# Hybrid decoder layer on one core: raw buffers of v by name and rising order, gate loads behind the first V products, two more U steps in the selection

## The chip, the cores and the metric

The kernel runs on one core of a Trainium2 chip. The metric is the device time of one execution in microseconds. The core has TensorE (PE, its weight loads as PEld), VectorE (DVE), ScalarE (ACT), GpSimd (POOL) and SyncE (SP), which here only issues DMAs. Each engine, and SyncE's DMA queue, works through its own instructions in order.

## The reference, cut to what matters

The layer first mixes tokens (two groups of mixers, of which nothing changes here) and then runs PEER: each of 512 tokens selects, for each of 8 heads, 16 of 16384 experts by product keys, and sums `gelu(x . u_i) * gate_i * v_i` over its 128 experts.

```python
s = jnp.einsum('thpd,hpkd->thpk', q, sub_keys).astype(f32)
top_s, top_i = lax.top_k(s, K)
cand_s = (top_s[:, :, 0, :, None] + top_s[:, :, 1, None, :]).reshape(T, H, K * K)
best_s, best_pos = lax.top_k(cand_s, K)
expert_idx = jnp.take_along_axis(cand_i, best_pos, axis=-1)
gate = jax.nn.softmax(best_s, axis=-1)
...
act = jnp.einsum('td,ted->te', x_blk, u[i_blk]).astype(f32)
hid = jax.nn.gelu(act, approximate=False) * g_blk
return jnp.einsum('te,ted->td', hid.astype(v.dtype), v[i_blk])
```

## The kernel before

Three of the four token tiles (384 tokens) are computed densely: for each of 128 blocks of 128 experts a U step makes all products of the block with the tokens, the gates (zero where an expert is not selected) multiply them, and a V step multiplies with v's block and adds up in PSUM. The fourth tile gathers its own rows of u and v with indirect DMAs (`gather`, on GpSimd's queue), and VectorE works them off (`use`).

Matrix products are made from a high and a low half of each operand, three matmuls for each product (`mm3`, lines 108 to 110). ScalarE makes the high half; the low half is a subtraction on VectorE, or on GpSimd where `split` is told so (line 104). A U step is `u_part` 0 to 7, three matmuls each. At part 0 and part 4 `rhs_part` asks for the load of the U block two steps on (`us.loads`, two raw buffers, tile ur) and splits half a block of the next one (tiles uh and ul). `keep` closes a step: gelu on ScalarE and, for tokens whose gates are there, a multiplication with the gate row in `ring`, on VectorE.

The order of the work is written out by hand, engine by engine. It has these stages here.

- The selection. VectorE finds the best keys and turns them to indices (`select`, one call for a tile of tokens, with a tree of additions over tile gat); `spread` transposes indices and gates on TensorE, `spread2` copies them out of PSUM. Between these calls stand U steps (`u_run`), and ScalarE writes broadcast copies (`ties`, `piece`). In this stage GpSimd makes the low halves of U.
- The gate stage, 48 units of 8 tokens (`gunit`). VectorE makes one-hot tiles A, eq and B (`gprep`), TensorE 16 matmuls of them (tile pg), which give the dense gates of 8 tokens for all 128 blocks. The gates of the first 59 blocks go to `ring` in SBUF, those of the other 69 to a stage buffer, which after every 8 units is written to DRAM (tile gd, a DMA of ScalarE's queue). Between the units stand U parts, spread evenly so that all but two of the steps up to block 58 are done at the end. In this stage VectorE makes the low halves of U.
- The turn. The pool with A, eq, B and the stage buffers is closed. A new one is opened over its memory (`vp`) for the halves of v, the halves of the gate rows (hh and hl) and four raw buffers of v (tile vr). Two U steps stand here (the two `u_run(1)`), the first loads and splits of v, and `hprep(0)`, which splits gate row 0.
- The loop over the blocks e = 0 to 127 of v. A step has six groups of V products (18 matmuls) and, as long as there are any, one U step, of block 59 + e (24 matmuls). `vs.loads(e + 4)` asks for the raw block four steps on, `gload` reads a gate row of a block from 59 on back from DRAM into the place in `ring` that is free. `vs.split`, `hprep` make the halves for the next step.

A raw buffer may be loaded again when both halves of the block in it have been made. A load into memory that another tile held before waits for the last user of that tile. All loads of u, v, gate rows and constants go through SyncE's queue, so each waits behind the ones issued before it.

Of the kernel before, what the change touches and what calls it, by code (L numbers as in the profile page):

```python
# [7 lines left out]
F32 = mybir.dt.float32  # L8
# [10 lines left out]
D = 1024  # L19
# [16 lines left out]
class Stream:  # L36
# [9 lines left out]

    def loads(s, upto):
        while s.nl <= min(upto, len(s.src) - 1):
            s.raw[s.nl] = s.c.tile([128, 1024], F32, name=s.nm + "r", bufs=s.nraw)
            s.y.load(s.raw[s.nl], s.src[s.nl])  # L50
            s.nl += 1

# [11 lines left out]
class Layer:  # L64
# [31 lines left out]
    def tt(self, out, x, y, op):  # L96
        return self.V.tensor_tensor(out, x, y, op=op)  # L97
# [758 lines left out]
    def experts(self):  # L856
# [4 lines left out]
        c = ctx.enter_context(tc.tile_pool(name="ex", bufs=1, reuse_waits="tile"))  # L861
        NE, RS = 128, RING
# [7 lines left out]
        us = self.us  # L870
# [99 lines left out]
        def piece():  # L970
            t, o, i = pieces.pop(0)
            act(o, i, AF.Copy)

        def select(t):

            while any(p[0] == t for p in pieces):
                piece()
            ii = kp.tile([128, 2, 8, 16], F32, name="ii", bufs=2)
            for e in range(2):
                oh = c.tile([128, 8, 16, 16], F16, name="gat", tag="gat", bufs=3)  # L980
                tt(oh, bc(CF[0][:, e, t], 2, 16), bc(itj if e else its, 1, 8), OP.is_equal if e else OP.is_ge)
                tt(oh, oh, TIE[t][:, e], OP.mult)
                for n in (8, 4, 2):
                    tt(oh[:, :, 0:n, :], oh[:, :, 0:n, :], oh[:, :, n:2 * n, :], OP.add)
                tt(ii[:, e], oh[:, :, 0, :], oh[:, :, 1, :], OP.add)
            IX[t] = ii
# [24 lines left out]
        def spread(t):  # L1011
            ii, g = IX.pop(t), bs[:, t]
            p = pt()
            T.transpose(p[:, 0:128], flat(ii[:, 0]), ident)
            T.transpose(p[:, 128:256], flat(ii[:, 1]), ident)
            T.transpose(p[:, 256:384], flat(g), ident)
            act(gs[:, 0, t * 128:(t + 1) * 128], p[:, 256:384], AF.Copy, scale=SC)
            SPR[t] = p
# [29 lines left out]
        def u_part(i, pool=False):  # L1048
            e = nu[0]
            if e >= NE:  # L1050
                return
            if i == 0:
                up[0] = pt()
            self.rhs_part(up[0][:, :TD], tsd, not hold[0] and nu[0] < RS - 4)
            if i in PP and pieces:
                piece()
            if i == 7:
                keep(e, up[0])
                nu[0] += 1

        def u_run(n):
            for _ in range(n):
                for i in range(8):
                    u_part(i)
# [27 lines left out]
        ties(2)  # L1092
        u_run(1)
        select(1)
        spread(0)
        u_run(1)
        ties(3)
        select(2)
        u_run(2)
# [4 lines left out]
        select(3)  # L1104
        u_run(2)
        spread(2)
        u_run(4)
        spread2(2)
        idx = c.tile([128, 128], I32, name="idx")
        gt0 = c.tile([128, 128], F32, name="gt0")  # L1110
# [118 lines left out]
        vp = ctx.enter_context(tc.tile_pool(name="vp", bufs=1, reuse_waits="tile"))  # L1229
        vs = Stream(self, vp, "v", [a["v"][e * 128:(e + 1) * 128, :] for e in range(NE)], 4)  # L1230
        HT[0] = htile()
        vs.loads(1)
        u_run(1)
        vs.split(1)
        hprep(0)
        u_run(1)
        vs.loads(3)

        g0 = ng[0]
        share = [0]  # L1240
# [6 lines left out]
        hs = {}  # L1247

        def gload(e):
            if e < NE:  # L1250
                load(ring[:, e % RS, :], gd3[:, e - RS, :])

        gload(RS)

        def final():

            nv = lambda: c.tile([128, 4], F32, name="rs3", bufs=4)
            hf = [slice(0, 512), slice(512, 1024)]
            junk = [c.tile([128, D], F32, name="gat", tag="gat", bufs=3), vp.tile([128, D], F32, name="vr", bufs=4)]
            v = [nv() for _ in range(4)]  # L1260

            def products(t):
                s = slice(t * 128, t * 128 + 128)
                for n in range(2):
                    for e in (NE - 2, NE - 1):
                        self.mm3(pv[t][n], HT[e][0][:, s], HT[e][1][:, s], *vs.parts[2 * e + n], False, e == NE - 1)

            def residual(t, n):
                h = hs[t][:, hf[n]]
                stt(h, pv[t][n], 1.0 / SC, h, OP.mult, OP.add)  # L1270
                square(t, n)

            def square(t, n):
                act(junk[t % 2][:, hf[n]], hs[t][:, hf[n]], AF.Square, accum_out=v[t][:, n:n + 1])

            def weight(t, n, eng):
                eng.tensor_tensor(hs[t][:, hf[n]], hs[t][:, hf[n]], wf[:, hf[n]], op=OP.mult)

            def mean(t):
                V.tensor_scalar(v[t][:, 2:3], v[t][:, 0:1], EPS * D, None, op0=OP.add)  # L1280
                V.tensor_scalar(v[t][:, 0:1], v[t][:, 1:2], v[t][:, 2:3], 1.0 / D, op0=OP.add, op1=OP.mult)

            def power(t):
                G.tensor_tensor(v[t][:, 3:4], v[t][:, 0:1], self.mhalf, op=OP.pow)

            def scale(t):
                stt(hs[t], hs[t], v[t][:, 3:4], wf, OP.mult, OP.mult)
                load(self.out[t], hs[t])

            square(3, 0)  # L1290
            square(3, 1)
            mean(3)
            power(3)
            for t in range(3):
                products(t)
            residual(0, 0)
            residual(0, 1)
            scale(3)
            mean(0)
            power(0)  # L1300
            residual(1, 0)
            weight(1, 0, G)
            residual(1, 1)
            weight(1, 1, G)
            scale(0)
            mean(1)
            power(1)
            residual(2, 0)
            weight(2, 0, G)
            residual(2, 1)  # L1310
            weight(2, 1, V)
            act(hs[1], hs[1], AF.Copy, scale=v[1][:, 3:4])
            load(self.out[1], hs[1])
            mean(2)
            power(2)
            act(hs[2][:, hf[0]], hs[2][:, hf[0]], AF.Copy, scale=v[2][:, 3:4])
            V.tensor_scalar(hs[2][:, hf[1]], hs[2][:, hf[1]], v[2][:, 3:4], None, op0=OP.mult)
            load(self.out[2], hs[2])

        for e in range(NE):  # L1320
            todo = [gather] * (plan[e + 1] - plan[e])
            pos = [(2 * i + 1) * 7 // max(1, 2 * len(todo)) for i in range(len(todo))]

            def fill(i, todo=todo, pos=pos):
                while pos and pos[0] <= i:
                    pos.pop(0)
                    todo.pop(0)()

            vs.loads(e + 4)
            if e == NE - 2:  # L1330

                hprep(e + 1)
                vs.split(2 * e + 2)
                vs.pair = us.pair
                vs.split(2 * e + 3)
                final()
                break
            hh, hl = HT.pop(e)

            def vgrp(n, t):  # L1340
                s = slice(t * 128, t * 128 + 128)
                vh, vl = vs.parts[2 * e + n]
                self.mm3(pv[t][n], hh[:, s], hl[:, s], vh, vl, e == 0, e == NE - 1)

            for i in range(3):
                vgrp(0, i)
                if i == 2:
                    vs.parts.pop(2 * e)
                    vs.split(2 * e + 2)
                    hprep(e + 1)  # L1350
                    gload(e + 1 + RS)
                u_part(i)
                fill(i)
            u_part(3)
            for i in range(3):
                vgrp(1, i)
                if i == 2:
                    vs.parts.pop(2 * e + 1)
                    vs.split(2 * e + 3)
                u_part(4 + i)  # L1360
                fill(3 + i)
            u_part(7)
            fill(6)
            if e == NE - 12:
                for t in (0, 1):
                    hs[t] = us.c.tile([128, D], F32, name="ur", bufs=2)
                    load(hs[t], self.hd[t])
            if e == NE - 4:
                while ng[0] < 256 or pend:
                    gather()  # L1370
                vs.loads(NE - 1)
                wf = c.tile([128, D], F32, name="gat", tag="gat", bufs=3)
                load(wf, a["w_norm_final"].to_broadcast([128, D]))
                hs[2] = c.tile([128, D], F32, name="gat", tag="gat", bufs=3)
                load(hs[2], self.hd[2])
                hs[3] = acc[0]
# [90 lines left out]
```

## Time and profile before

| | us |
|---|---|
| median of 3 runs | 1524.52 |
| lowest, highest | 1524.38, 1526.88 |
| profiled execution, its own time | 1525.01 |
| its span in the trace | 1523.2 |
| TensorE busy in the span | 1479.2 (97%) |
| VectorE busy | 1168.4 (77%) |
| ScalarE busy | 632.3 (42%) |
| GpSimd busy | 451.6 (30%) |

The profile comes from one execution. Its own time contains the span, from the first instruction to the last, and about 1.8 us around it. Matmuls are pipelined, so the busy time of TensorE says when it had work, not that it ran at its peak. Idle time in front of an instruction stands in square brackets with what ended it. A q behind an engine's name means its queue or sequencer.

### The profile page before, as it was taken

How to read it: one execution, taken by the hardware profiler on the slowest of the kernel's cores; microseconds unless marked ns; L12 is line 12 of the kernel's file. 1: busy time of each engine (PE TensorE's matmuls, PEld its weight loads, DVE VectorE, ACT ScalarE, POOL GpSimd, SP SyncE). 2: the span in 40 equal slices, each digit the busy share in tenths (PEclk: the TensorE clock that was granted, in tenths of full speed). 3: DMA queues.
4: the chain of work that ended last, by engine and by line, in shares of the span. 5: the costliest groups of instructions: out<-in, count | busy, mean ns of one | idle time of the engine just before them, and what ended most of it. 6: DMA issues, size and time to landing. Idle time of an engine off the chain costs nothing.

```text
span 1523.2 us, 22401 instructions
## 1 busy us (share of the span) xinstructions
PE 1479.2 (97%) x7904; PEld 1290.1 (85%) x7904; DVE 1168.4 (77%) x2473; ACT 632.3 (42%) x1201; POOL 451.6 (30%) x380
## 2 busy tenths in 40 slices
PE   7999999999988999989999999999999999999997
PEld 6777767888988999878999999999889998888886
DVE  6543654599999999977777777787788788888886
ACT  5335633433653544433333333333333333444444
POOL 1002403444564000002333333333243333334332
PEclk9999999999999999999999999999999999999999
DMA  5231213322334556658889888889889897888894
GB/s 186 83 125 56 70 53 131 108 84 90 105 110 140 157 150 169 180 180 301 317 304 322 317 307 303 318 309 316 297 317 316 314 322 257 293 301 301 298 327 178
DMA packets 148738, 335.56 MB, mean 220 GB/s; under 512 B 64640, under 2 KB 73872, under 8 KB 148496
## 3 DMA queue, kind: packets, MB, share of 16 engines
q1 hardware_dynamic: 58672, 186.32, 36.0%
q0 software_dynamic: 36864, 134.23, 24.6%
q10 hardware_dynamic: 53088, 13.57, 3.8%
q8 instruction: 62, 1.02, 0.3%
q14 instruction: 52, 0.43, 0.1%
HBM read 315.79 MB, written 18.28 MB: 219 GB/s over the span
## 4 chain that ended last, share of the span: by engine, by line
PE 53%; issue 20%; DVE 13%; POOL 9%; DMA 3%; ACT 2%; POOLq 0%; SPq 0%; DVEq 0%; ACTq 0%
PE pm L108 16%; PE pm L109 16%; PE pm L110 16%; POOL gat L1133 8%; DVE gat L97 4%; PE pg L1184 2%; DVE ul L104 1%; DVE B L97 1%; PE pm L902 1%; DMA gd<-stage 1%; DVE ring L97 1%; DVE eq L97 1%; DVE A L97 1%; ACT b L91 1%; DMA gat<-in_u,idx 1%
## 5 line engine op out<-in xcount | busy, mean ns | idle before, releaser
L108 PE MATMUL pm<-nT,uh 128*128 128x384 f32 (+1 forms) x1152 | 404.3, 351 | 8.6 <-ACT uh L91 8.1
L109 PE MATMUL pm<-nT,uh 128*128 128x384 f32 (+1 forms) x1152 | 399.1, 346 | 0.5 <-DVE nT L97 0.5
L110 PE MATMUL pm<-nT,ul 128*128 128x384 f32 (+1 forms) x1152 | 397.5, 345 | 1.1 <-POOL ul L104 0.9
L109 PE MATMUL pm<-vl,hh 128*128 128x512 f32 x765 | 301.5, 394 | 1.2 <-DVE vl L104 1.2
L110 PE MATMUL pm<-vh,hl 128*128 128x512 f32 x765 | 300.9, 393 | 0.0
L108 PE MATMUL pm<-vh,hh 128*128 128x512 f32 x765 | 300.6, 393 | 0.2 <-ACT vh L91 0.2
L1133 POOL DMA_INDIRECT gat<-in_u,idx x128 | 137.8, 1076 | 477.6 <-DVE gat L100 470.3
L91 ACT ACTIVATE uh<-ur 128x512 fp32r<-128x512 f32 x288 | 180.2, 629 | 219.3 <-PE pm L109 185.9
L108 PEld LDWEIGHTS pm<-nT,uh 128*128 128x128 f32 x1152 | 218.0, 189 | 34.3 <-ACT uh L91 8.6
L109 PEld LDWEIGHTS pm<-nT,uh 128*128 128x128 f32 x1152 | 217.7, 189 | 25.4 <-DVE nT L97 1.1
L110 PEld LDWEIGHTS pm<-nT,ul 128*128 128x128 f32 x1152 | 217.8, 189 | 8.7 <-POOL ul L104 2.6
L1133 POOL DMA_INDIRECT gat<-in_v,idx x128 | 148.4, 1159 | 256.1 <-DVE n2a L100 223.1
L91 ACT ACTIVATE vh<-vr 128x512 fp32r<-128x512 f32 x255 | 159.5, 626 | 136.9 <-PE pm L110 136.9
L104 DVE TENSOR_TENSOR vl<-vr,vh 128x512 fp32r<-128x512 f32 x255 | 175.2, 688 | 33.5 <-ACT vh L91 33.0
L104 DVE TENSOR_TENSOR ul<-ur,uh 128x512 fp32r<-128x512 f32 x206 | 140.7, 689 | 61.5 <-ACT uh L91 61.3
L100 DVE SCALAR_TENSOR_TENSOR n2a<-gat,dots,n2a 128x1024 f32<-128x1024 f32 x128 | 163.9, 1280 | 24.2 <-DMA gat<-in_v,idx 19.2
L110 PEld LDWEIGHTS pm<-vh,hl 128*128 128x128 f32 x765 | 143.5, 188 | 32.7 <-DVE hl L104 0.3
L100 DVE SCALAR_TENSOR_TENSOR gat<-gat,n2a 128x1024 f32<-128x1024 f32 x128 | 156.1, 1220 | 13.9 <-DMA gat<-in_u,idx 13.7
L109 PEld LDWEIGHTS pm<-vl,hh 128*128 128x128 f32 x765 | 143.9, 188 | 15.6 <-DVE vl L104 1.9
L108 PEld LDWEIGHTS pm<-vh,hh 128*128 128x128 f32 x765 | 144.0, 188 | 14.2 <-ACT vh L91 0.7
L104 POOL TENSOR_TENSOR ul<-ur,uh 128x512 fp32r<-128x512 f32 x82 | 116.5, 1427 | 101.3 <-ACT uh L91 101.2
L91 ACT ACTIVATE gl<-pm 128x384 f32<-128x384 f32 (+16 forms) x104 | 46.0, 442 | 223.8 <-PE pm L110 223.8
(254 smaller groups left out, 1709.2 us busy)
## 6 DMA issues: line engine op xcount, KB each, us to landing
ur<-in_uT SPq DMA_DIRECT2D x128, 512.0 KB, 5.9
vr<-in_v SPq DMA_DIRECT2D x128, 512.0 KB, 5.5
gd<-stage ACTq DMA_DIRECT2D x6, 2208.0 KB, 14.7
ring<-gd SPq DMA_DIRECT2D x69, 192.0 KB, 5.6
wraw<-in_w_in SPq DMA_DIRECT2D x23, 512.0 KB, 4.3
ur<-in_w_query SPq DMA_DIRECT2D x16, 512.0 KB, 3.6
b<-in_x SPq DMA_DIRECT2D x8, 512.0 KB, 3.7
wraw<-in_w_out SPq DMA_DIRECT2D x8, 512.0 KB, 3.9
```

Source lines behind the costliest of these rows:

```text
L91: return self.S.activation(out, in_, f, **k)
L97: return self.V.tensor_tensor(out, x, y, op=op)
L100: return self.V.scalar_tensor_tensor(out, x, s, y, op0=op0, op1=op1, **k)
L104: (self.G if pool else self.V).tensor_tensor(lo, src, hi.bitcast(F32), op=OP.subtract)
L108: T.matmul(out, lhi, rhi, start=start, stop=False)
L109: T.matmul(out, lhi, rlo, start=False, stop=False)
L110: T.matmul(out, llo, rhi, start=False, stop=stop)
L902: T.matmul(p[:, t * 128:(t + 1) * 128], q[:, t * 128:(t + 1) * 128], skT[:, b, :], start=True, stop=True)
L1133: G.indirect_dma_start(out=r, out_offset=None, in_=src, in_offset=bass.IndirectOffsetOnAxis(ap=idx[:, k:k + 1], axis=0))
L1184: T.matmul(o, A[:, t // 2, :, t % 2], B[:, i, t // 2, :, t % 2], start=i == 0, stop=i == 1)
```

## The change

The raw buffers of v and u get names of their own (vr0 to vr3, ur0 and ur1), each with one buffer, in place of one name with four or two buffers; two users at the end follow. Three blocks of v are asked for ahead of the two U steps of the turn, in place of two ahead and two behind; step 0 asks for none beyond them, and step 1 then asks for blocks 3 to 5. The gate rows 59 and 60 are read back near the end of step 0, in place of row 59 ahead of the loop and row 60 in the middle of step 0. In the selection, the U step behind `spread(0)` is put ahead of it and one more with it, and the last run has five steps for four; the gate stage, which does what is left up to block 56, then has two steps less.

```diff
     def loads(s, upto):
         while s.nl <= min(upto, len(s.src) - 1):
-            s.raw[s.nl] = s.c.tile([128, 1024], F32, name=s.nm + "r", bufs=s.nraw)
+            s.raw[s.nl] = s.c.tile([128, 1024], F32, name=f"{s.nm}r{s.nl % s.nraw}", bufs=1)
             s.y.load(s.raw[s.nl], s.src[s.nl])
...
         select(1)
+        u_run(2)
         spread(0)
-        u_run(1)
         ties(3)
...
         spread(2)
-        u_run(4)
+        u_run(5)
         spread2(2)
...
         HT[0] = htile()
-        vs.loads(1)
+        vs.loads(2)
         u_run(1)
         vs.split(1)
         hprep(0)
         u_run(1)
-        vs.loads(3)
...
-        gload(RS)
-
...
-            junk = [c.tile([128, D], F32, name="gat", tag="gat", bufs=3), vp.tile([128, D], F32, name="vr", bufs=4)]
+            junk = [c.tile([128, D], F32, name="gat", tag="gat", bufs=3), vp.tile([128, D], F32, name=f"vr{NE % 4}", bufs=1)]
...
-            vs.loads(e + 4)
+            vs.loads(e + 4 if e else 2)
...
-                    gload(e + 1 + RS)
+                    if e:
+                        gload(e + 1 + RS)
...
+            if e == 0:
+                gload(RS)
+                gload(RS + 1)
             u_part(7)
...
-                    hs[t] = us.c.tile([128, D], F32, name="ur", bufs=2)
+                    hs[t] = us.c.tile([128, D], F32, name=f"ur{t}", bufs=1)
```

## Rows read from the trace of the kernel before

**Rows 1.** Stretches: busy time (instructions) of each engine, granted clock, DMA share, GB/s.

```profile
core 0: us, PE busy (x) PEld busy (x) DVE busy (x) ACT busy (x) POOL busy (x), PEclk, DMA share, GB/s
395.71:475.23 79.52, 70.13 (x388) 67.30 (x388) 77.21 (x117) 44.16 (x70) 52.32 (x34) 0.98 0.37 119
475.23:481.49 6.26, 5.84 (x35) 5.56 (x35) 4.31 (x8) 2.07 (x4) 1.75 (x2) 0.73 0.76 253
481.49:555.70 74.21, 73.59 (x617) 70.05 (x617) 70.40 (x132) 38.35 (x90) 0.00 (x0) 1.00 0.53 154
555.70:666.48 110.78, 106.90 (x880) 100.55 (x880) 109.58 (x194) 52.07 (x129) 1.15 (x1) 1.00 0.54 155
...
687.89:692.30 4.41, 4.41 (x12) 3.71 (x13) 4.40 (x8) 2.41 (x5) 0.55 (x1) 0.55 1.02 389
692.30:1096.00 403.70, 403.70 (x2011) 364.01 (x2010) 313.92 (x535) 147.16 (x286) 134.06 (x126) 1.00 0.88 309
```

**Rows 2.** Timeline of TensorE: start, duration, instruction, idle time before it.

```profile
687.89 0.69 PE L108 MATMUL pm<-nT,uh 128*128 128x384 f32 x1 [8.12 <-ACT uh L91]
...
706.02 0.39 PE L108 MATMUL pm<-vh,hh 128*128 128x512 f32 x1
```

**Rows 3.** Timeline of ScalarE at the turn.

```profile
668.88 0.52 ACTq L1197 DMA_DIRECT2D gd<-stage  x1
...
687.21 1.15 ACT L91 ACTIVATE uh<-ur 128x512 fp32r<-128x512 f32 x2 [10.32 <-DMA ur<-in_uT]
```

**Rows 4.** Timeline of SyncE's queue at the turn, successive issues merged.

```profile
664.94 17.64 SPq L88 DMA_DIRECT2D vr<-in_v  x2
682.67 0.86 SPq L88 DMA_DIRECT2D ur<-in_uT  x2
...
684.69 0.44 SPq L88 DMA_DIRECT2D ring<-gd  x1
```

**Rows 5.** Waits of SyncE's queue, 655 to 730: total, times, longest.

```profile
SPq L88 <- DMA gd<-stage: 16.9, 1, 16.9
```

**Rows 6.** Timeline of VectorE at the turn and in the loop's step 1.

```profile
670.17 0.69 DVE L104 TENSOR_TENSOR ul<-ur,uh 128x512 fp32r<-128x512 f32 x1 [0.66 <-ACT uh L91]
...
698.30 0.56 DVE L97 TENSOR_TENSOR ring<-gl,ring 128x384 f32<-128x384 f32 x1 [1.81 <-ACT gl L91]
...
700.57 0.69 DVE L104 TENSOR_TENSOR vl<-vr,vh 128x512 fp32r<-128x512 f32 x1
```

**Rows 7.** Tile ur, 604 to 605: one U load beside a write of 601.8.

```profile
DMA to landing us min/median/max: 7.0/7.0/7.0
```

**Rows 8.** Tile stage, 475 to 660: the earlier writes, issue to landing.

```profile
DMA to landing us min/median/max: 14.3/14.7/15.1
```

**Rows 9.** The page's DMA issues: count, KB each, median us to landing.

```profile
ring<-gd SPq DMA_DIRECT2D x69, 192.0 KB, 5.6
```

**Rows 10.** Timeline of ScalarE: the closings of two successive U steps.

```profile
467.81 0.49 ACT L91 ACTIVATE ring<-pm 128x384 f32<-128x384 f32 x1 [1.56 <-PE pm L110]
...
471.97 0.49 ACT L91 ACTIVATE ring<-pm 128x384 f32<-128x384 f32 x1 [1.56 <-PE pm L110]
```

**Rows 11.** Timeline of TensorE: first transposes of the selection, first gate product.

```profile
421.71 0.27 PE L1014 MATMUL pm<-ident,ii 128*128 128x128 f32 x1
...
475.23 0.23 PE L1184 MATMUL pg<-B,A 128*128 128x128 f16 x1 [3.30 <-DVE B L97]
```

**Rows 12.** Timeline of VectorE in the selection: two trees of three additions.

```profile
435.58 1.48 DVE L97 TENSOR_TENSOR gat<-gat 128x1024 f16<-128x1024 f16 x3
...
441.88 4.41 DVE L97 TENSOR_TENSOR gat<-gat 128x1024 f16<-128x1024 f16 x3
```

**Rows 13.** Timeline of GpSimd over the same trees.

```profile
437.24 1.29 POOL L104 TENSOR_TENSOR ul<-ur,uh 128x512 fp32r<-128x512 f32 x1 [2.77 <-ACT uh L91]
439.08 7.06 POOL L104 TENSOR_TENSOR ul<-ur,uh 128x512 fp32r<-128x512 f32 x4 [0.55 <-ACT uh L91]
```

**Rows 14.** VectorE's groups, 481.49 to 666.48: count, busy us, mean ns, idle before.

```profile
L104 DVE TENSOR_TENSOR ul<-ur,uh 128x512 fp32r<-128x512 f32 x63 | 41.9, 684 | 5.3 <-ACT uh L91 5.1
```

## The prediction

> **What bounds the kernel now.** I read the table of stretches first, then TensorE's gaps, then the queue that ended the largest of them, then the two stages that receive or lose U steps.
>
> The stretches [rows 1] show four regimes. From 395.71 to 475.23 (the selection) VectorE is busy 77.21 of 79.52 us and TensorE 70.13: VectorE sets the pace. From 481.49 to 555.70 (the first 19 gate units) TensorE is busy 73.59 of 74.21 us: TensorE sets it. From 555.70 to 666.48 (the next 27) it is VectorE, 109.58 of 110.78. From 692.30 on, in the loop over the 128 blocks of v, TensorE has no idle time (403.70 of 403.70), so what it gains or loses before that point reaches the end one to one.
>
> Between the gate stage and that loop TensorE stands still for 8.12 us until ScalarE has made the high half of a U block [rows 2]. ScalarE had itself waited 10.32 us for that block's load [rows 3]. The load was issued only at 682.67, right behind two loads of v that took SyncE's queue from 664.94 to 682.58 [rows 4]; 16.9 us of that is a wait for the write of the last stage buffer to DRAM [rows 5], issued at 668.88 [rows 3]. One raw buffer of v lies on memory that this write still reads, and the in-order queue holds the U load behind it. After the gap the granted clock is 0.55 for 4.41 us [rows 1], between the two levels of 1.2 and 2.4 GHz: 4.41 x 0.45 = 1.98 us more. The turn costs 8.12 + 1.98 = 10.1 us.
>
> **The change part by part.** *Placement and order of v's raw buffers.* By the tile sizes, the closed gate pool holds per partition A 2 x 2 KB, eq 2 KB, B 2 x 4 KB, then two stage buffers of 17.25 KB: the last one lies at 31.25 to 48.5 KB. The pool that follows holds 12 KB of halves of v, 6 KB of halves of gates, then four raw buffers at 18, 22, 26 and 30 KB. Only the one at 30 touches the last stage. In rising order, blocks 0 to 2 need not wait, and three loads go out at about 664.9, 665.3 and 665.7. The U load behind them then waits only for its own buffer, whose last reader is the low half made from 670.17 [rows 6]: issue at about 670.9. It runs beside the stage write; a U load 3 us behind an earlier such write landed after 7.0 us [rows 7]. That is 677.9, then some 0.6 us for a high half (1.15 for two [rows 3]) and 0.69 for a low one [rows 6]: 679.2, against a last product that ended at 687.89 - 8.12 = 679.77. So I take the whole stall away: **-10.1 us**. A landing 4 us later would leave some 4 us of it: bounds -6 to -10.1. What could be late next is the following U load; its buffer frees one U step later (4.16 us, below), at about 675, and with 5 to 7 us for it the load is there at 682, a whole step before TensorE reads it.
>
> *Blocks 3 and 4 of v in step 1.* Block 3 still waits for the stage write, but is split only in step 2, two steps after step 0. A step has 42 products (24 of U, 18 of v) and 2011 of them took 403.70 us [rows 1], so 8.43 us a step; I cost the move at nothing. Renaming the U buffers and the two final ones changes no order that I can see: nothing.
>
> *Gate loads behind the first products.* Row 59 of the gates is read back once the stage write has landed. Earlier writes took 14.3 to 15.1 us [rows 8]: 683.2 to 684.0. Two more v blocks, 1 MB, now share the DMA engines with it, at 389 GB/s [rows 1] up to 2.8 us: 686.8 at most. With 5.6 us for the read [rows 9] the row lands between 688.8 and 692.4. Its user is the multiplication that closes U step 59, on VectorE at 698.30 before [rows 6] and, 10.1 us earlier, at 688.2 now. This is a new wait of 0.6 to 4.2 us; queued behind it on VectorE are low halves of U, gather products and the low half of v that was made from 700.57 to 701.26 [rows 6] and read first at 706.02 [rows 2], a cover of 4.8 us. On SyncE the read-back holds block 3 and the next U load, wanted a full step later. Cost 0; without that cover up to 4.2 us.
>
> *Two U steps moved into the selection.* A step is 4.16 us of TensorE (two successive closings lie at 467.81 and 471.97 [rows 10]), two ScalarE high halves and two low halves, which GpSimd makes here and VectorE in the gate stage.
>
> On TensorE the steps fit into waits: between the first transposes at 421.71 and the first gate product at 475.23 it ran ten steps, 41.6 of 53.5 us, with 3.30 us of waiting at the end alone [rows 11]; twelve are 49.9. On VectorE they don't come free. The three additions of the tree take 1.48 us at 435.58 [rows 12], when GpSimd is idle (its next split starts at 437.24 after 2.77 us idle [rows 13]), and 4.41 us at 441.88 [rows 12], when GpSimd runs four splits in a row [rows 13]: 2.93 us for three additions that met a split, 0.98 each. Four more splits cost 4 x 0.98 = 3.9 us on the engine that sets this stage. Bounds: 0, if all four fall beside instructions that read PSUM, to 3.9.
>
> The Trainium skill (SBUF — State Buffer, Who interferes with whom) says that a VectorE instruction with two SBUF inputs and a GpSimd one that reads SBUF exclude each other for a whole instruction, so it speaks against this part. By it, each split could hold VectorE for its whole 1.29 us, 5.2 us in all, and the sum below would end 1.3 us higher; the row's 0.98 decides.
>
> Against this, the wait of 3.30 us before the first gate product [rows 11] shrinks: TensorE's twelve steps end no earlier than 421.7 + 49.9 = 471.6 plus what waits and transposes remain, VectorE's part at 475.2 + 3.9 = 479.1, and of the 11.9 us that TensorE lost in this stretch I leave it six or seven. With it goes the clock dip of the first unit, 0.73 over 6.26 us [rows 1], 1.7 us. Selection and first unit: 3.9 - 1.7 = **+2.2 us**. Upper bound: the dip stays and a second one of the same size follows a longer wait at the later transposes, 3.9 + 1.7 = 5.6. Lower: -1.7.
>
> *The gate stage with two steps less.* It runs 31 steps for 33, 248 parts for 264. Sixteen parts of 0.52 us are 8.3 us of TensorE over 48 units, 0.173 each. In the 19 units that TensorE sets this is 3.3 us; VectorE was idle 3.8 us there [rows 1], so it doesn't take the place. In the 27 that VectorE sets, only its own work counts: four low halves of 41.9/63 = 0.665 us [rows 14], 2.7 us over 48 units, 1.5 here. Fewer closing multiplications and longer gate multiplications nearly cancel. Sum **-4.8 us**; bounds -2.7 (VectorE sets all) and -8.3 (TensorE sets all).
>
> **Sum.** -10.1 + 2.2 - 4.8 = -12.7, on the profiled execution's 1525.01: 1512.3 us. That execution is 0.5 us above the median shown, 1524.52; I don't correct for it. A measurement here can tell 0.2%, about 3 us, from no change.
>
> **The rivals.** *The U steps cost more than they free* (0.17): more collisions, both dips, and a gate stage that VectorE sets throughout. The selection's VectorE share speaks for it, the two waits of TensorE against it: -10.1 + 5.6 - 2.7 = -7.2, 1517.8 us. *TensorE decides everywhere* (0.10): splits beside instructions that don't collide and the full 8.3 back: -10.1 - 8.3 = -18.4, 1506.6. The idle 1.2 us of VectorE in the last 27 units speak against it. *The change doesn't do what it says* (0.08): the first three buffers are placed otherwise, or the U load still lands late, and the stall stays: 2.2 - 4.8 = -2.6, 1522.4, within 0.2%. For it: the addresses are worked out from code, not seen. Against: before, just one of the first two v loads waited [rows 4, 5]. *Slower* (0.05): the read-back of gate row 59 blocks VectorE. Each microsecond by which it lands after 688.2 + 4.8 = 693.0 stalls TensorE one; the gain is gone at 693.0 + 12.7 = 705.7, and 3 us later the kernel is slower by more than 0.2%, 40 us after the write was issued. No write in the trace took over 15.1.
>
> **How the numbers follow.** My forecast has 0.60 and gives 1512.3 us. The range takes in most of its terms' bounds and both other cases that end faster, but for the last half microsecond of the second: 1507 to 1518.5. Left out are the last two rivals, 0.13, and that edge, under 0.2 together. Faster 0.87 (forecast and first two rivals), same 0.08, slower 0.05.
>
> **What would show it.** Right: three v loads issued by 666.5 after the same stretch, no TensorE wait over 1 us between gate stage and v loop, no clock dip there; four more GpSimd splits in the selection, its VectorE stretch about 4 us longer, the first units of the gate stage some 0.17 us shorter; a VectorE wait of 1 to 4 us for the gate row at the end of step 0 that TensorE doesn't feel. Wrong: SyncE still waiting for the stage write ahead of a U load, a TensorE gap in step 1 or 2 of the v loop, or a selection longer by more than the gate stage gets shorter.

## The result, and the profile after

The changed kernel takes 1505.75 us (median of 4 runs, 1503.4 to 1506.71), the kernel before 1524.45 beside it (4 runs, 1524.38 to 1526.88): ratio 0.9889, 95% interval 0.9863 to 0.9915. The forecast was faster, 1512.3 with a range from 1507.0 to 1518.5. The sign was right, the size too small: 18.7 us are gone where 12.7 were forecast, and the median lies 1.25 us below the low end. The ratio is not the quotient of the two medians (0.9877); on 1524.45 it gives 1507.5 us. The same kernel run once more (label after_again) took 1507.63 against 1523.38, 15.8 us less. The profiled execution took 1506.71 us, its span 1504.9, against 1525.01 and 1523.2.

The table of stretches of the changed kernel, cut at the places that answer to those of [rows 1]: the selection up to the first gate product, its first unit, the next 19, the next 27, the turn, step 0 of the loop, steps 1 to 48, step 49, and steps 50 to 67.

```profile
core 0: us, PE busy (x) PEld busy (x) DVE busy (x) ACT busy (x) POOL busy (x), PEclk, DMA share, GB/s
395.70:478.77 83.07, 77.74 (x436) 74.10 (x435) 80.76 (x117) 47.31 (x76) 58.96 (x37) 1.00 0.37 120
478.77:483.42 4.65, 4.26 (x35) 3.98 (x34) 4.24 (x8) 2.06 (x4) 3.29 (x3) 1.00 0.80 247
483.42:554.93 71.51, 70.72 (x599) 66.98 (x599) 69.29 (x129) 36.49 (x87) 0.00 (x0) 1.00 0.57 166
554.93:663.92 108.99, 103.17 (x849) 95.67 (x849) 108.01 (x191) 50.05 (x125) 1.14 (x1) 1.00 0.53 153
663.92:676.34 12.42, 12.07 (x81) 11.95 (x80) 9.28 (x17) 6.08 (x12) 1.01 (x1) 1.00 1.06 329
676.34:684.66 8.32, 8.32 (x44) 7.53 (x43) 6.39 (x12) 3.21 (x6) 1.15 (x1) 1.00 0.98 279
684.66:1084.02 399.36, 399.36 (x2018) 361.49 (x2017) 312.46 (x536) 149.33 (x289) 134.49 (x125) 1.00 0.90 319
1084.02:1094.29 10.27, 8.94 (x44) 7.54 (x43) 10.27 (x14) 3.21 (x6) 5.30 (x4) 1.00 0.74 259
1094.29:1246.21 151.92, 151.92 (x758) 136.95 (x757) 121.76 (x156) 55.89 (x108) 52.30 (x48) 1.00 0.88 312
```

Steps 1 to 48 of the loop in the kernel before, the same columns; the row in [rows 1] runs across other borders.

```profile
697.57:1102.69 405.12, 405.12 (x2017) 365.25 (x2017) 313.29 (x534) 149.00 (x289) 133.52 (x125) 1.00 0.88 310
```

Both rows hold the same 48 steps, TensorE has no idle time in either and the granted clock is 1.00 in both, the upper of its two levels of 1.2 and 2.4 GHz. Yet a step takes 405.12/48 = 8.440 us before and 399.36/48 = 8.320 us after. That is the part that was not forecast. Behind step 49 the changed kernel runs at 151.92/18 = 8.440 as well.

The turn: SyncE's queue and ScalarE's first high halves of the U block that was late.

```profile
662.37 1.33 SPq L88 DMA_DIRECT2D vr<-in_v  x3
668.31 9.02 SPq L88 DMA_DIRECT2D ur<-in_uT  x3
683.19 0.80 SPq L88 DMA_DIRECT2D ring<-gd  x2
684.04 1.60 SPq L88 DMA_DIRECT2D vr<-in_v  x3
```
```profile
675.01 1.16 ACT L91 ACTIVATE uh<-ur 128x512 fp32r<-128x512 f32 x2 [0.70 <-DMA ur<-in_uT]
```

Three loads of v leave in 1.33 us where two held the queue for 17.64 [rows 4]; the U load goes out at 668.31, not 682.67, and ScalarE waits 0.70 us for it, not 10.32 [rows 3]. The wait of SyncE's queue for the stage write is 5.8 us now and stands before the gate rows only. VectorE's multiplication with the gate row that is read back:

```profile
686.91 0.56 DVE L97 TENSOR_TENSOR ring<-gl,ring 128x384 f32<-128x384 f32 x1 [2.19 <-DMA ring<-gd]
```

A new wait of 2.19 us, inside the forecast's 0.6 to 4.2, and TensorE doesn't feel it. TensorE's own waits from 400 to 1300, whole list (total, times, longest):

```profile
PE pg L1184 <- DVE B L97: 8.0, 23, 1.2
PE pm L110 <- POOL ul L104: 2.7, 4, 0.7
PE pm L109 <- DVE vl L104: 1.3, 1, 1.3
PE pm L1015 <- DVE ii L97: 1.3, 1, 1.3
```

The 8.12 us of [rows 2] are not among them. The one wait in the loop, 1.3 us for a low half of v, is in step 49: VectorE stood 5.3 us for the residual row of the fourth token tile there (tile n2a, loaded just when it is wanted). It was there before as well.

The two profiled executions, term by term:

| | before | after | difference | forecast |
|---|---|---|---|---|
| first gate product at | 475.23 | 478.77 | +3.54 | +3.9 |
| first unit | 6.26 | 4.65 | -1.61 | -1.7 |
| next 19 units | 74.21 | 71.51 | -2.70 | -3.3 |
| next 27 units | 110.78 | 108.99 | -1.79 | -1.5 |
| turn and step 0 | 31.09 | 20.74 | -10.35 | -10.1 |
| steps 1 to 48 | 405.12 | 399.36 | -5.76 | 0 |
| step 49 | 9.92 | 10.27 | +0.35 | 0 |
| sum | | | -18.32 | -12.7 |

The rows of steps 1 to 48 and of step 49 are what the forecast lacks; the others sum to -12.91.

### The profile page after: what moved, and what is told of

The parts are those of the page before. It is cut to its first block, busy times and chain, and to the rows that moved or that the text cites. A ratio compares the mean times of both kernels' runs of the same rounds, so it can differ in the third digit from the quotient of the medians.

```text
span 1504.9 us, 22404 instructions
## 1 busy us (share of the span) xinstructions
PE 1471.1 (98%) x7904; PEld 1282.7 (85%) x7904; DVE 1168.5 (78%) x2467; ACT 632.2 (42%) x1199; POOL 460.5 (31%) x384
## 4 chain that ended last, share of the span: by engine, by line
PE 52%; issue 20%; DVE 14%; POOL 9%; DMA 3%; ACT 2%; POOLq 0%; DVEq 0%; SPq 0%; ACTq 0%
PE pm L109 15%; PE pm L108 15%; PE pm L110 15%; POOL gat L1133 9%; DVE gat L97 4%; DVE ul L104 1%; DVE B L97 1%; DMA ur<-in_uT 1%; PE pg L1184 1%; DVE eq L97 1%; DVE ring L97 1%; DVE A L97 1%; PE pm L902 1%; ACT b L91 1%; DMA gat<-in_u,idx 0%
## 5 line engine op out<-in xcount | busy, mean ns | idle before, releaser
L91 ACT ACTIVATE uh<-ur 128x512 fp32r<-128x512 f32 x288 | 180.5, 629 | 202.7 <-PE pm L109 176.7
L109 PEld LDWEIGHTS pm<-vl,hh 128*128 128x128 f32 x765 | 143.7, 188 | 15.8 <-DVE vl L104 2.2
L104 POOL TENSOR_TENSOR ul<-ur,uh 128x512 fp32r<-128x512 f32 x86 | 124.3, 1453 | 100.0 <-ACT uh L91 92.7
L91 ACT ACTIVATE gl<-pm 128x384 f32<-128x384 f32 (+15 forms) x102 | 45.4, 445 | 221.3 <-PE pm L110 221.3
```

The lines of the kernel that those rows point to most:

```text
L91: return self.S.activation(out, in_, f, **k)
L104: (self.G if pool else self.V).tensor_tensor(lo, src, hi.bitcast(F32), op=OP.subtract)
L109: T.matmul(out, lhi, rlo, start=False, stop=False)
```

## The experiments

The question is where the loop's second rate comes from. Theory A: the wait at the turn leaves TensorE in a slower rhythm, and any wait does. Theory B: the rate comes with the two U steps that were moved. Theory C: it has to do with what changes at step 49, where the gathers go from u to v. The kernel before, run beside each group of four, had medians of 1522.36 (14 runs, 1514.81 to 1528.45), 1524.02 (7 runs) and 1523.38 (13 runs).

**The turn alone** (label turn_only): all of the change but the moved steps.

```diff
         select(1)
-        u_run(2)
         spread(0)
+        u_run(1)
...
         spread(2)
-        u_run(5)
+        u_run(4)
```

> The changed kernel with the selection of before: only the buffers, loads and gate loads of the turn are changed. Both theories take the 10.3 us of the turn away. Theory A (the loop's faster rate of 8.32 us a step is kept when TensorE enters the loop without a wait): the steps run at 8.32 us, 49 of them, and the kernel ends at about 1508.4 us, 2.6 us above the changed kernel. Theory B (the rate hangs on the edits in the selection, or on chance): steps at 8.44 us and about 1514 us.

1509.85 us (5 runs), ratio 0.991 (0.9878 to 0.9942). Steps 1 to 48:

```profile
689.53:1088.89 399.36, 399.36 (x2018) 361.49 (x2017) 315.78 (x539) 149.24 (x289) 136.51 (x126) 1.00 0.90 320
```

The rate of 8.320 comes without the U steps: B is out. The profiled execution took 1507.41; this one had no wait in step 49 and went on at 8.320 to the end of the mixed steps.

**The U steps alone** (label usteps_only): the kernel before with the two steps moved.

```diff
         select(1)
+        u_run(2)
         spread(0)
-        u_run(1)
...
         spread(2)
-        u_run(4)
+        u_run(5)
```

> The kernel before with the two U steps moved and nothing else. The wait of 8 us at the turn stays. From the two traces the selection should end 3.5 us later, the first unit be 1.6 us shorter and the other units 4.5 us shorter in sum: -2.6 us, about 1521.9 us. Theory A: the loop's steps stay at 8.44 us. Theory B: they fall to 8.32 us and the kernel ends at about 1516 us.

1518.34 us (10 runs), ratio 0.9987 (0.9962 to 1.0012): by its interval no difference from before, so the time can't tell A's 1521.9 from B's 1516; the steps of the profiled execution can. Step 0, steps 1 to 48, steps 50 to 67:

```profile
673.64:692.36 18.72, 10.62 (x43) 9.00 (x43) 7.11 (x12) 4.25 (x8) 1.91 (x2) 0.73 0.91 306
692.36:1091.72 399.36, 399.36 (x2017) 361.49 (x2017) 313.36 (x534) 149.01 (x289) 133.12 (x125) 1.00 0.88 314
1101.16:1253.08 151.92, 151.92 (x757) 136.93 (x757) 121.68 (x157) 56.11 (x108) 51.35 (x48) 1.00 0.89 313
```

The stall is there (18.72 us for a step), and the loop runs at 8.320 behind it all the same; after a wait of 0.5 us in step 49 it runs at 151.92/18 = 8.440. So theory A falls in its plain form: a wait doesn't always leave the slower rate.

**A wait in the middle of the loop** (label stall24): the changed kernel, with scratch work on VectorE ahead of the v split of step 24.

```diff
+                    if e == 24:
+                        dly = vp.tile([128, D], F32, name="dly", bufs=1)
+                        V.memset(dly, 0.0)
+                        for _ in range(5):
+                            stt(dly, dly, 1.0, dly, OP.mult, OP.add)
                     vs.split(2 * e + 2)
```

> The changed kernel with some 6.5 us of extra VectorE work (on a scratch tile, not part of the result) ahead of the split of v in step 24, so that TensorE waits once, 1 to 2 us, near step 25. Theory A (a wait of TensorE leaves the slower rate behind): 8.32 us a step up to 24, 8.44 us from 25 or 26 on, and the profiled span 4 to 5 us longer, about 1509 to 1510. Theory C (the rate goes with the gathers of u or v, and the switch at step 49 is theirs): the steps go back to 8.32 us after the wait, and only the wait itself is added, 1 to 2 us.

1513.47 us (one run). TensorE waited 3.8 us in step 25, not the 1 to 2 expected. Steps 1 to 24 and 26 to 67:

```profile
684.95:884.63 199.68, 199.68 (x1010) 180.74 (x1009) 158.53 (x270) 74.58 (x144) 68.84 (x63) 1.00 0.91 324
898.48:1252.96 354.48, 354.48 (x1766) 319.52 (x1765) 279.44 (x423) 130.45 (x253) 117.87 (x110) 1.00 0.89 312
```

199.68/24 = 8.320 and 354.48/42 = 8.440: the rate turns at the wait, with the gathers still on u. C is out.

**No wait in step 49** (label acc_early): the changed kernel, with the residual row loaded at step 8 into a tile of its own.

```diff
+            if e == 8:
+                acc2[0] = vp.tile([128, D], F32, name="acc", bufs=1)
+                load(acc2[0], self.hd[GT])
...
-                    acc[0] = c.tile([128, D], F32, name="n2a", tag="n2a", bufs=1)
-                    load(acc[0], self.hd[GT])
+                    acc[0] = acc2[0]
```

> The changed kernel with the residual of the gathered tile loaded into a buffer of its own in step 8, in place of a load at step 49 into a buffer that comes free there. TensorE's wait at step 49 (1.95 us more than a step) should go. Theory A: with no wait the rate of 8.32 us holds to the last U step, 19 steps more at 0.12 us: -1.95 - 2.3 = -4.2 us, about 1501.5 us. Theory C: the rate changes to 8.44 us at the switch from gathers of u to gathers of v all the same: about -1.9 us, 1503.9 us.

1504.03 us (4 runs), ratio 0.9877 (0.9839 to 0.9915); the profiled execution 1503.03. Steps 1 to 48 and 49 to 68:

```profile
685.24:1084.60 399.36, 399.36 (x2018) 361.54 (x2018) 316.67 (x541) 149.06 (x289) 137.16 (x127) 1.00 0.90 321
1084.60:1250.99 166.39, 166.39 (x841) 150.63 (x841) 133.91 (x171) 60.99 (x118) 56.38 (x54) 1.00 0.88 309
```

166.39/20 = 8.320: without the wait the rate stays. Against the changed kernel's profiled execution that is 3.7 us less; the medians, 1505.75 and 1504.03, are too near to each other for their intervals to part them, and 1504.03 alone would speak for C's 1503.9 rather than A's 1501.5. The rate of the steps decides it.

The four together gave a new theory. **Theory D**: TensorE has two rhythms for this loop, keeps the one it has as long as it doesn't wait, and at a wait falls into either.

**Several waits** (label waits8): the kernel with the residual row loaded early and the scratch work at eight steps.

```diff
+        LATE = {8: 3, 16: 6, 24: 3, 32: 6, 40: 3, 48: 6, 56: 3, 64: 6}
...
+                    if e in LATE:
+                        for _ in range(LATE[e]):
+                            stt(dly, dly, 1.0, dly, OP.mult, OP.add)
```

> The changed kernel with the residual row of the last stage loaded early (so that step 49 has no wait of its own), and with scratch work on VectorE ahead of the v split of eight steps (8, 16, ... 64): about 3 us of it in every other one, about 6.5 us in the others, so that TensorE waits about 1 us and about 4 us in turn. Theory D (the rate of the mixed loop is taken anew at each wait and kept until the next one): the steps between two waits run at 8.32 or at 8.44 us, some of the stretches at each. Theory A (after any wait the loop is at the slow rate for good): 8.32 up to the first wait and 8.44 in every stretch behind it. Theory E (only a wait that is long enough to be followed by a dip of the granted clock changes the rate): no change after the waits of 1 us. Time by D about 1503 + 8 x 3 = 1527, give or take 5.

1527.22 us (one run). Only the four larger delays reached TensorE, as waits of 2.46, 2.33, 4.85 and 3.08 us in steps 17, 33, 49 and 65; the smaller ones VectorE made up, but for 0.37 us more in step 9, behind which the rate stayed. Steps 10 to 16, 18 to 32, 34 to 48 and 50 to 64:

```profile
760.57:818.80 58.23, 58.23 (x295) 52.71 (x295) 48.36 (x79) 21.69 (x42) 20.77 (x19) 1.00 0.94 331
831.71:958.31 126.60, 126.60 (x632) 114.12 (x631) 104.41 (x172) 46.49 (x90) 42.66 (x39) 1.00 0.89 313
969.46:1094.26 124.80, 124.80 (x631) 112.98 (x631) 102.23 (x170) 46.80 (x91) 43.83 (x40) 1.00 0.90 317
1109.44:1236.04 126.60, 126.60 (x632) 114.12 (x631) 104.95 (x132) 46.49 (x90) 43.58 (x39) 1.00 0.88 312
```

8.32, 8.44, 8.32, 8.44 us a step. A wait brings the loop back to the faster rate as well, which A can't give and D can. Theory E looks right in this run: the granted clock of the step with the wait was 0.87, 0.89 and 0.87 in steps 17, 49 and 65, with 8.44 behind them, and 1.00 in steps 9 and 33, with 8.32 behind them. The other runs take it away. The U steps alone came out of a step 0 with a granted clock of 0.73 at 8.32, and turned to 8.44 at step 49, behind 0.5 us of waiting with the clock at 1.00.

**The order of products** (labels grouped_acc and grouped_waits): three groups of V products, four U parts, three groups, four parts, in place of one and one; the second kernel has the scratch work too.

```diff
...
-                u_part(i)
-            u_part(3)
+            for i in range(4):
+                u_part(i)
...
```

> The changed kernel with the residual row loaded early, and the products of one loop step put in another order: three groups of V products, four U parts, three groups of V products, four U parts, so that TensorE goes from one width of product to the other 4 times a step and not 12 times. If a change of width is what costs (16 cycles of 2.4 GHz each at the step of 8.320 us, 8.24 us being the 42 products alone): the step falls to 8.24 + 4 x 0.0067 = 8.267 us, 68 steps give 3.6 us, the time is about 1500.5 against 1504 with the early load alone. Rival: the cost doesn't hang on the changes of width, and the step stays at 8.32 (1504). A second rival: the four U parts in a row make the hand-over of their sums to VectorE late, waits appear in each step, and the time is above 1504.

> The order of products with 4 changes of width a step, with the residual row early and the same scratch work on VectorE ahead of the v split of eight steps as in the run with 12 changes. If the two rates of the loop are two costs of a change of width (16 or 40 cycles of 2.4 GHz each): the stretches between the waits run at 8.267 or at 8.307 us a step, a third of the difference of 0.12 us that 12 changes show. Rival: the second rate has to do with something else that goes on in a step, and the stretches differ by 0.12 us as before, or not at all.

1504.2 us (4 runs), ratio 0.9871 (0.9849 to 0.9892), and 1528.68 (one run). Steps 1 to 48 of the first; steps 10 to 16, 18 to 32 and 34 to 48 of the second, behind waits of 1.38, 2.90 and 4.16 us:

```profile
687.24:1087.56 400.32, 400.32 (x2018) 363.49 (x2017) 312.02 (x539) 153.17 (x289) 144.09 (x126) 1.00 0.89 320
```
```profile
762.22:820.60 58.38, 58.38 (x295) 53.02 (x295) 47.67 (x79) 21.90 (x42) 22.12 (x19) 1.00 0.92 332
832.35:957.45 125.10, 125.10 (x632) 113.60 (x631) 102.54 (x173) 47.05 (x90) 48.02 (x40) 1.00 0.89 318
972.01:1097.11 125.10, 125.10 (x631) 113.59 (x631) 102.92 (x170) 47.70 (x91) 45.96 (x39) 1.00 0.88 316
```

All are 8.340 us a step, and so are the steps behind the three waits that follow. In both, the price of a change of width falls as the cause, and the rival holds but for 0.02 us: a third of the changes doesn't cost a third, and the stretches don't differ at all. The second rate was seen only in the order of one group of V products and one U part in turn. That the other order can't have it is not shown by six waits: at odds of 9 in 13 (below), six in a row come out alike about one time in nine.

**The selection's splits** (label selv): the changed kernel, with the low halves of U made by VectorE from the first search tree on. This and the next two test the other term that could have been luck, 0.98 us of VectorE for a split on GpSimd.

```diff
-            self.rhs_part(up[0][:, :TD], tsd, not hold[0] and nu[0] < RS - 4)
+            self.rhs_part(up[0][:, :TD], tsd, not hold[0] and nu[0] < RS - 4 and not onv[0])
...
+        onv[0] = True
         select(0)
```

> The changed kernel in its own order, with one thing altered: from the first search tree to the first gate product the low halves of the U splits (30 of them) are made by VectorE and not by GpSimd. By the forecast's price a split on GpSimd holds VectorE up by 0.98 us; on VectorE itself it takes 0.68 us (the median of these splits in the trace of the rearranged selection). So 30 x 0.30 = 9 us: the first gate product at about 470 us instead of 478.77, and the time at about 1497 against 1505.75. Rival: the splits on GpSimd run beside VectorE and cost it little; then 30 x 0.68 = 20 us are added, and the time is about 1526.

1528.92 us (10 runs), ratio 1.0037 (1.0016 to 1.0059). The first gate product came at 504.95. Three of TensorE's four longest waits in the selection:

```profile
423.82 0.69 PE L110 MATMUL pm<-nT,ul 128*128 128x384 f32 x1 [9.29 <-DVE ul L104]
...
442.54 0.69 PE L110 MATMUL pm<-nT,ul 128*128 128x384 f32 x1 [3.75 <-DVE ul L104]
...
475.80 0.69 PE L110 MATMUL pm<-nT,ul 128*128 128x384 f32 x1 [4.95 <-DVE ul L104]
```

Neither expectation had this. The split stands behind a whole tree on VectorE's queue, TensorE waits for it and then runs its block of U steps while VectorE waits in turn: the engines alternate. The 1526 of the rival is met, its reason is not. What the run does show is VectorE's trees without GpSimd beside them: their 48 instructions take 33.2 us here, against 59.5 in the changed kernel (rows in the next experiment), with nothing altered but where the splits are made.

**The selection rearranged** (label mixed): the parts of eleven U steps run between the stages of the trees, the splits are VectorE's, and three steps go back to the gate stage. And the same with the splits on GpSimd (label mixed_pool).

```diff
+            def mix(j):
+                while done[0] * 12 < total * j:
+                    u_part(mp[0] % 8)
+                    mp[0] += 1
+                    done[0] += 1
...
+                mix(6 * e + 2)
-                for n in (8, 4, 2):
+                for x, n in enumerate((8, 4, 2)):
...
+                    mix(6 * e + 3 + x)
```

> The changed kernel with its selection rearranged: the parts of eleven U steps run between the stages of the search trees, not in blocks behind them, and the low halves of their splits are made by VectorE, not by GpSimd; three steps go back into the gate stage. In the profiled run a split on GpSimd ran into VectorE's trees and cost 0.98 us of the path each; on VectorE the same split is 0.61 to 0.67 us. Theory (the selection is VectorE's own work plus these collisions): the first gate product comes some 12 to 18 us earlier, the gate stage takes back three steps' worth, 8 to 10 us, and the time is 1498 to 1503, against 1505.75. Rival: TensorE's products now stand between the trees on VectorE's queue, the one waits for the other at each place, and the time is 1506 or more.

> The rearranged selection (the parts of eleven U steps between the stages of the search trees, three steps back in the gate stage), but with the low halves of the splits left to GpSimd. If the gain of the rearranged kernel (first gate product at 465.30 us, loop at 670.84) comes from where the splits are made: 24 splits x 0.30 us = 7 us of it go, the first gate product comes at about 472 us and the time is about 1504. Rival: it comes from the order, TensorE's products standing between the trees; then the first gate product stays within 2 us of 465.3 and the time near 1497.

Mixed: 1494.68 us (4 runs, 1493.82 to 1496.97), ratio 0.9812 (0.9792 to 0.9832). With GpSimd: 1506.84 (4 runs), ratio 0.9883 (0.9853 to 0.9912). VectorE's groups of the trees from 395.7 to 475 us (instructions, busy us, mean ns, idle before), of the changed kernel and of the rearranged one:

```profile
L97 DVE TENSOR_TENSOR gat<-gat 128x1024 f16<-128x1024 f16 (+2 forms) x24 | 25.9, 1077 | 0.8
L97 DVE TENSOR_TENSOR gat<-gat,k 128x2048 f16<-128x2048 f16 x8 | 17.3, 2160 | 0.6
L97 DVE TENSOR_TENSOR gat<-tops,itj 128x2048 f16<-128x2048 f16 x4 | 6.0, 1489 | 0.0
L97 DVE TENSOR_TENSOR gat<-tops,its 128x2048 f16<-128x2048 f16 x4 | 6.0, 1488 | 0.0
L97 DVE TENSOR_TENSOR ii<-gat 128x128 f32<-128x128 f16 x8 | 4.3, 536 | 0.3
```
```profile
L104 DVE TENSOR_TENSOR ul<-ur,uh 128x512 fp32r<-128x512 f32 x27 | 18.5, 686 | 2.8 <-ACT uh L91 2.7
L97 DVE TENSOR_TENSOR gat<-gat 128x1024 f16<-128x1024 f16 (+2 forms) x24 | 11.2, 468 | 0.5
L97 DVE TENSOR_TENSOR gat<-gat,k 128x2048 f16<-128x2048 f16 x8 | 9.7, 1218 | 0.0
L97 DVE TENSOR_TENSOR gat<-tops,its 128x2048 f16<-128x2048 f16 x4 | 4.9, 1218 | 0.0
L97 DVE TENSOR_TENSOR gat<-tops,itj 128x2048 f16<-128x2048 f16 x4 | 4.9, 1219 | 0.0
L97 DVE TENSOR_TENSOR ii<-gat 128x128 f32<-128x128 f16 x8 | 2.3, 286 | 0.1
```

The same 48 instructions take 59.5 us with the splits on GpSimd and 33.0 with them on VectorE. GpSimd made 29 splits from 410 to 476: 26.5/29 = 0.91 us for each, against the forecast's 0.98. On VectorE itself a split takes 0.686. GpSimd loses time too. Its splits of the changed kernel from 410 to 476, and those from 300 to 395, ahead of the trees (duration ns, minimum, median and maximum):

```profile
L104 POOL TENSOR_TENSOR ul<-ur,uh 128x512 fp32r<-128x512 f32 x29 | 48.5, 1688 | 19.0 <-ACT uh L91 11.8 <-PE pm L110 5.5 <-PE pm L109 1.5
```
```profile
L104 POOL TENSOR_TENSOR ul<-ur,uh x32: 1282/1292/1302, 302.6 to 393.3; 128x512 fp32r<-128x512 f32 x32
```

A split takes 1.69 us beside the trees and 1.29 before them, 0.40 more. Against the changed kernel run in the same group (1507.63, label after_again), the order alone gives nothing clear of noise (1506.84) and the splits on VectorE alone lose 21 us (1528.92). Both together, run in another group, lie 11 to 13 us below the changed kernel's two medians (1505.75 and 1507.63): VectorE's splits pay only where TensorE's products stand between the trees. The 1498 to 1503 expected of both was missed by 3 us; the profiled execution, 1496.97, had no wait in step 49 and kept 8.320 to the last U step. The first gate product came at 465.30 (GpSimd: 475.69), and the stretch from there to the loop grew by 205.54 - 197.57 = 8.0 us for the three steps; both are as expected, but that 24 splits were to cost 7 us more on GpSimd and cost 10.4.

**Both** (label best): the rearranged selection and the early load of the residual row.

> The rearranged selection with the splits on VectorE, and the residual row of the last stage loaded early: both together. In the profiled run of the rearranged selection alone no step of the loop waited, so the early load has little left to give: 1493 to 1496 against 1494.68. If step 49 waits in its other runs, up to 2 us more are gained.

1495.03 us (4 runs), ratio 0.9803 (0.9773 to 0.9833). No more than the rearranged selection alone, whose profiled execution had no wait in step 49 either.

**Once more** (label after_again): the changed kernel beside these.

> The changed kernel once more, on the chip of the three above and against the same runs of the kernel before. The first 49 steps of the loop follow on products without a wait, so they run at 8.320 us; step 49 waits for the residual row, and the steps behind it run at 8.320 or at 8.440 us. Time 1503 to 1507, and within 0.3% of 0.989 of the kernel before.

1507.63 us (4 runs), ratio 0.9891 (0.986 to 0.9922); the ratio is as expected, the time 0.6 us above. Step 49 took 8.965 us, its second product being late. Steps 1 to 48, and 50 to 67:

```profile
685.75:1085.11 399.36, 399.36 (x2017) 361.49 (x2017) 313.41 (x535) 149.40 (x289) 134.50 (x125) 1.00 0.90 319
1094.08:1246.00 151.92, 151.92 (x758) 136.93 (x757) 121.80 (x157) 55.80 (x108) 51.35 (x48) 1.00 0.89 312
```

## Why the prediction was right in its terms and too small in its sum

**The turn** held: three loads at once, no TensorE wait, no dip of the clock, -10.35 against -10.1. The turn alone takes the stall away without the U steps.

**Selection and first unit** held, +3.54 and -1.61. From the first tree to the first gate product it is 64.6 us before and 64.4 with the turn alone, 68.4 in the changed kernel and with the U steps alone, so +3.8 comes with these steps; the price rested on three additions of one tree [rows 12, 13], was one for an addition and was taken as one for a split, and stands at 0.91 for the whole stage. The first unit's gain comes with them as well: TensorE waits 3.3 us ahead of the first gate product before and with the turn alone, and 1.2 and 1.1 us in the changed kernel and with the U steps alone. The rule of the Trainium skill that was named in the prediction (SBUF — State Buffer, Who interferes with whom) agrees with the runs in kind: the same two-input instructions of VectorE take 33.0 us without GpSimd's splits beside them and 59.5 with them. Its whole 1.29 us for each split is more than the 0.91 that VectorE lost; with the 0.40 by which a split itself grew it comes to 1.31.

**The gate stage** held: -4.49 in the two stretches against -4.8. **The gate row** landed as foreseen, 2.19 us late for VectorE and for nobody else.

**The step that failed**, the term put at nothing, is the one in the first part: "From 692.30 on, in the loop over the 128 blocks of v, TensorE has no idle time (403.70 of 403.70), so what it gains or loses before that point reaches the end one to one." And with it the 8.43 us a step that the second part took as the loop's own. TensorE was busy all the time at the full clock, and still not at its fastest: the same products take 8.320 or 8.440 us a step. The removal of the stall did more than take 10.1 us from the turn; it let TensorE enter the loop without a wait, and all ten profiled executions in which it did so with this order of products ran at 8.320 up to the first wait. Of the thirteen stretches of the loop behind a step that TensorE could not run through (the stall at the turn twice, step 49 five times, scratch work six times), nine ran at 8.440 and four at 8.320. The wait of 1.3 us in step 49 of the kernel with VectorE's splits (label selv) is among the four. In the profiled pair the faster rate is worth 48 x 0.12 = 5.76 us, and -12.91 - 5.76 + 0.35 = -18.32. The rival that TensorE decides everywhere has the same number, -18.4, by chance: its 8.3 us from the gate stage were 4.49, and its free splits cost 3.54 less 1.61.

That makes part of the gain a matter of odds: by these counts an execution of the kernel before may fall into the faster rate after the stall, as the one with the U steps alone did. The other runs of the kernel before were not profiled, so that their spread (13.6 us over 14 runs) comes from this is argued, not shown; and 68 steps of 0.12 us make 8.2 us, so the two rates can't be all of it.

What the two rhythms are inside TensorE stays open. The records show no idle time, the clock is the same, and in a step of either rate ScalarE's first instruction stands 0.20 us behind its start. But the starts of the products say where the 0.12 us lies (means over steps 1 to 48, changed kernel and kernel before). From the first to the second of the three U matmuls of a product it is 172.1 and 176.7 ns, from the second to the third 173.9 and 177.3; with V, 229.1 and 233.5, then 232.5 and 233.3. From a U to a V matmul it is 173.3 and 174.8, from V to U 232.5 and 235.0. Summed over a step, some 97 of 121 ns lie between matmuls of one width and 24 at the twelve changes. So the slower rhythm is not a dearer change of width, and is not one place in the step either.

## What to carry to other kernels

A stretch in which an engine shows no idle time is not thereby at a fixed rate: divide it by its steps and compare that with the same products elsewhere, or with another execution, before taking it as a constant. A stall ahead of a long loop may cost more than its own length, because of the rhythm in which TensorE comes out of it. And an operation given to GpSimd because it is idle has a price on VectorE; ask what it costs there (0.91 us here) and what it would take on VectorE itself (0.69 us), and then whether VectorE's order lets it go there.

## What the runs showed of the hardware that was not expected

- One order of matmuls, with no idle time of TensorE and the clock at 1.00, ran at 8.320 or at 8.440 us for 42 products; in every profiled execution the rate stayed until a product next came late, and a wait of 2.33 us brought the faster one back. With the products in blocks of nine and twelve it was 8.340 after each of six waits.
- The additions of the tree take 468 ns each on average without GpSimd's splits beside them and 1077 with them.
- A split on GpSimd beside the trees cost VectorE 0.91 us and took 0.40 us longer itself, where alone it takes 1.29.
- Moving splits from GpSimd to VectorE lost 21 us in one order of the program (1507.63 to 1528.92) and gained 12 in another (1506.84 to 1494.68).
